# A hybrid decoder trunk on one core: byte distances of split weights, and a shorter lead of the slabs that are split ahead of a norm

## The chip, the cores and the metric

The kernel runs on 1 core of one Trainium2 chip. The metric is the device time of one execution in microseconds (us). The engines are named as the profile names them: PE is TensorE's matmul, PEld its weight load, DVE is VectorE, ACT is ScalarE, POOL is GpSimd, SP is SyncE, which issues most DMAs.

## The reference

`x` is 256 tokens x 1024 features. There are two layers of three sub-layers each: a SwiGLU FFN, a mixer, another FFN. Layer 0's mixer is a hybrid of a state-space scan and forgetting attention; layer 1's is a gated linear recurrence.

```python
def swiglu(x, w_in, w_out):                       # w_in 1024 x 5632, w_out 2816 x 1024
    gate, up = jnp.split(x @ w_in, 2, axis=-1)
    return (jax.nn.silu(gate) * up) @ w_out

def recurrent_mixer(h, w_in, conv_w, conv_b, w_a, b_a, w_x, b_x, lam, w_out):
    gate, xr = jnp.split(h @ w_in, 2, axis=-1)
    gate = jax.nn.gelu(gate, approximate=True)
    xr = causal_conv(xr, conv_w, conv_b)
    return (rg_lru(xr, w_a, b_a, w_x, b_x, lam) * gate) @ w_out

# every sub-layer, with weight 0.5 for the FFNs and 1 for the mixers
x = x + weight * rms_norm(f(rms_norm(x, g_pre)), g_post)
```

The hybrid mixer projects h to z, xbc, dt, q, k, v and f with one matrix of 1024 x 5656, runs a chunked scan on the first three and 8 attention heads on the others, and projects the 2048 results back with `hyb_w_out`.

## The kernel before

**Products from parts.** A float32 operand is split in two float32r parts: hi is the rounded copy, lo the rest. A product is hi x hi + hi x lo + lo x hi, three matmuls of 128 x 128 stationary columns and up to 512 moving columns. ACT makes hi (`act.copy`, L268), DVE makes lo (L269).

**Slabs.** All weights come as slabs of 128 x 1024 (512 KB) in the order in which they are used (`order`, built from `plans`). SP loads a slab into one of five `raw` buffers (L249), then `prepare` splits it into a slot of `w`. A slot holds the hi part from its first element and the lo part `pitch` elements further (L263 to L266). There are seven slots; later output slabs go to a pool of the phase. `slabs` splits 5 or 6 slabs beyond those that an operation needs (`LOOKAHEAD`), unless a norm is under way.

**Activations.** `xT` holds the normed activations transposed, per feature block a hi and a lo part of 256 tokens each. In the built program `xT` begins at byte 25760 of each partition and the seven slots of `w` at 62624 and every 8704 bytes on. All of these leave 160 when divided by 256.

**Phases.** The six sub-layers run one after another. An FFN has 22 feature tiles f. The first three (`NA`) are done per token tile t = 0, 1 with `xT` stationary (kind A). From f = 3 on (kind B, `b_tiles`) the weights are stationary: 2 matmuls hi x (hi and lo), 512 columns; 16 lo x hi, 256 columns; 14 hi x (hi and lo). After each B come output steps of earlier tiles (kind O, `out_step`), 6 matmuls of 512 columns per token tile. The hybrid mixer has 8 tiles with `xT` stationary (V, `a_one`) and 36 slabs with the weights stationary (XBC, Z, Q, K, `b_one`), 24 matmuls of 256 columns each. The recurrent one has 8 of the first kind (RA) and 8 of the second (GATE).

**The end of a phase.** Output steps of token tile 0 come first; then `finish` records tile 0's post-norm, its residual sum and the next phase's pre-norm (L331 squares on ACT, L379, L382 and L347 on DVE, two small steps on POOL), while PE does the deferred output steps of tile 1. Before the norm, `finish` splits the slabs of the next phase's first 2 x NA operations, which are the six slabs of f = 0, 1, 2, and makes the norm's instructions stand behind the last split on each engine (`behind(..., firsts)`). Later on PE transposes the normed tile (L143), and ACT and DVE write it into `xT` (L312).

**Order.** PE's order is that of the code. On the other engines a scheduler orders the recorded instructions by priority; `tc.high_priority(offset=...)` brings some forward.

**The recurrence.** `lru(n0)` handles four of eight blocks. After the square root it multiplies (L948), scans (L950), applies GELU to the gate (L953), multiplies by it (L954) and splits the result into a slot of `w`, called `two` (L955 to L956), for the output steps. It does so first for n0 = 0, then for n0 = 4.

Of the kernel before, what the change touches and what calls it, by code (L numbers as in the profile page):

```python
# [8 lines left out]
F32 = mybir.dt.float32  # L9
F32R = mybir.dt.float32r  # L10
# [6 lines left out]
P = 128  # L17
# [8 lines left out]
NEG = -1e30  # L26
SLAB = 1024

STEP, PLACES = 8, 16

NA = 3
BEHIND = 2
# [70 lines left out]
def slabs_of(op):  # L103
    kind, ph = op[0], op[1]
    if kind in ("A", "B", "V", "RA"):
        return [(kind if kind in ("V", "RA") else "I", ph, op[2], j) for j in range(2)]
    if kind in ("DTF", "XBC", "Z", "Q", "K", "GATE", "O"):
        return [(kind, ph, op[2])]
    return []
# [6 lines left out]
def hybrid_trunk(ctx: ExitStack, tc: tile.TileContext, x_in, norm_g, ffn_in, ffn_out,  # L116
# [119 lines left out]
    def behind(ins, firsts):  # L236

        for h in firsts:
            if h.ins.engine == ins.ins.engine:
                tc.add_manual_dep(ins.ins, h.ins.name, mybir.DependencyInfo(  # L240
                    mybir.DependencyClass.NoSync, mybir.DependencyReason.DATA), reason="norms and splits in turn")
        return ins
# [9 lines left out]
    def prepare(n):  # L252
        while ready[0] < min(n, len(order)):
            key = order[ready[0]]
            late = is_late(key)
            if late and key[1] not in pools:
                break
            ready[0] += 1
            load(ready[0])
            raw, width = loaded[ready[0] - 1]  # L260
            slots = SPLIT if not late else 7 if PHASES[key[1]][0] == "ffn" else LATE[PHASES[key[1]][0]]

            pitch = SLAB + (STEP * (key[2] % PLACES) if key[0] == "I" and key[2] >= NA else 0)  # L263
            full = (pools[key[1]] if late else wp).tile([P, 2 * SLAB + (0 if late else STEP * PLACES)], F32R, name="w", bufs=slots)
            w = full[:, 0:2 * SLAB].rearrange("p (j c) -> p j c", j=2)
            w = [full[:, 0:SLAB], full[:, pitch:pitch + SLAB], w]  # L266
            c = slice(0, width)
            splits[:] = [behind(act.copy(w[0][:, c], raw[:, c]), hold)]  # L268
            splits.append(behind(dve.tensor_tensor(w[1][:, c], raw[:, c], w[0][:, c].bitcast(F32), op=ALU.subtract), hold))  # L269
            split[key] = w  # L270
            load(ready[0] + RAW)
# [86 lines left out]
        norms.discard((ph, t))  # L358
        normed.add((ph, t))

    def new_xT():
        return res.tile([P, KT, 2, NT * P], F32R, name="xT")

    def finish(ph, t, acc, weight):

        xt = xs[t]
        last = ph == len(PHASES) - 1
        upto = [where[k] for op in (plans[ph + 1][:2 * NA] if not last else []) for k in slabs_of(op)]
        prepare(max(upto, default=0) + 1)
        with tc.high_priority(offset=400):  # L370
            firsts = splits + hold
            ms = mean_square(acc, weight, firsts)
            r = work.tile([P, 1], F32, name="r", bufs=4)
            rstd_of(r, ms, weight)
            hg = []
            for h in range(2):
                cols = slice(h * 512, (h + 1) * 512)
                hg.append(work.tile([P, 512], F32, name="xn", bufs=3))
                behind(dve.tensor_tensor(hg[h], acc[h], state["g_post"][:, cols], op=ALU.mult), firsts)  # L379
            for h in range(2):  # L380
                cols = slice(h * 512, (h + 1) * 512)
                dve.scalar_tensor_tensor(  # L382
                    xt[:, cols], hg[h], r, xt[:, cols], op0=ALU.mult, op1=ALU.add)
                if last:
                    (sp, act)[h].dma_start(out[t * P:(t + 1) * P, cols], xt[:, cols])
        if not last:
            if t == 0:
                state["xT_next"] = new_xT()
            spawn(pre_norm(ph + 1, t, state["xT_next"], LAG["norm"]))

    gsrc = [(0, 0), (0, 2), (0, 4), (1, 0), (1, 2), (1, 4)]
# [60 lines left out]
        hold[:] = latest.values()  # L452
        start_pool.__exit__(None, None, None)

    xT = new_xT()
    first_norms(xT)

    def out_step(accs, k, t, n, act_hl, w, halves=(0, 1)):
# [153 lines left out]
    def run_hyb(ph, plan, xT, mp):  # L612
# [5 lines left out]
        act.dma_start(gs, ssm_g)  # L618
        cs = mp.tile([P, 64], F32, name="cs")
        dt = mp.tile([P, NT, 24], F32, name="dt")  # L620
        dec = mp.tile([P, HEADS], F32, name="dec")
        rows = tc.dram_tile([24, 256], F32, name="rows")

        at_pool = tc.tile_pool(name="at", bufs=1)
# [259 lines left out]
    def run_rec(ph, plan, xT, mp):  # L884
# [31 lines left out]
        def lru(n0):  # L916
# [28 lines left out]
                yield 0.5  # L945

            rooted[n0] = behind(act.activation(r, r, func=AF.Sqrt, scale=0.25), [squared[4]])
            dve.tensor_tensor(r, r, i, op=ALU.mult)  # L948
            for j in range(4):
                dve.tensor_tensor_scan(i[:, j, :], a[:, j, :], r[:, j, :], 0.0, op0=ALU.mult, op1=ALU.add)  # L950
            while ("gate", n0 + 3) not in done or 4 not in rooted:
                yield 0.5
            behind(act.activation(gt[:, nn, :], gt[:, nn, :], func=AF.Gelu_apprx_tanh), [rooted[4]])  # L953
            dve.tensor_tensor(gt[:, nn, :], gt[:, nn, :], i, op=ALU.mult)  # L954
            two = wp.tile([P, 2, 4, 256], F32R, name="w", bufs=SPLIT)  # L955
            split_to(two[:, 0, :, :], two[:, 1, :, :], gt[:, nn, :])  # L956
            parts.update((n0 + j, [two[:, k, j, :] for k in range(2)]) for j in range(4))
            done.update(("out", n) for n in range(n0, n0 + 4))

# [115 lines left out]
```

## Time and profile before

| what | value |
|---|---|
| time, median of 3 runs | 1052.2 us (1052.01 to 1052.62) |
| time of the profiled execution | 1055.53 us |
| its span in the profile | 1053.3 us |
| TensorE busy | 1035.5 us, 98% |
| VectorE, ScalarE busy | 719.0 us (68%), 597.6 us (57%) |
| DMA | 195.90 MB, mean 186 GB/s |
| matmuls of 256 columns, xT moving | 2272 |
| matmuls of 512 columns, xT moving | 1216 |

[...] What a matmul costs is read from start to start.

### The profile page before, as it was taken

The numbers are of one execution on the slowest core, as the hardware profiler recorded it, in microseconds if no ns is written. First come the engines' busy times: TensorE is split into PE (matmuls) and PEld (weight loads), VectorE is DVE, ScalarE is ACT, GpSimd is POOL, SyncE is SP. The second block draws the span as 40 slices with busy tenths as digits, with TensorE's granted clock in tenths as the row PEclk, the third lists the DMA queues.
The fourth block names the chain that finished last, engine by engine and source line by source line (L and its number), as shares of the span: only waits on it lengthen the run. The fifth ranks groups of instructions, "written<-read, shape, count | busy, mean of one in ns | idle before, by whom it ended". The sixth has DMA issues, their size and how long they took to land.

```text
span 1053.3 us, 16022 instructions
## 1 busy us (share of the span) xinstructions
PE 1035.5 (98%) x6084; PEld 911.4 (87%) x6084; DVE 719.0 (68%) x1156; ACT 597.6 (57%) x1060; POOL 24.5 (2%) x60
## 2 busy tenths in 40 slices
PE   8999999999999999999999999999999989999997
PEld 7888888999999988888888888888899878888886
DVE  7766557589888776855557685555769858655563
ACT  6755456455565566645546564454659847545551
POOL 1000000100000001000000100000010010000000
PEclk9999999999999999999999999999999999999999
DMA  7966656265645472856556285555735446665521
GB/s 270 319 215 193 195 185 211 68 229 178 207 148 160 139 251 98 297 194 194 185 180 220 81 294 189 181 193 193 229 107 190 146 160 239 217 200 177 187 81 40
DMA packets 55745, 195.90 MB, mean 186 GB/s; under 512 B 6972, under 2 KB 8148, under 8 KB 55668
## 3 DMA queue, kind: packets, MB, share of 16 engines
q1 hardware_dynamic: 52464, 190.04, 55.3%
q10 hardware_dynamic: 3204, 4.84, 1.4%
q8 instruction: 47, 0.77, 0.3%
q14 instruction: 30, 0.25, 0.1%
HBM read 193.78 MB, written 1.07 MB: 185 GB/s over the span
## 4 chain that ended last, share of the span: by engine, by line
PE 88%; DVE 4%; ACT 4%; issue 2%; POOL 1%; DMA 1%; POOLq 0%; DVEq 0%; ACTq 0%
PE rot L139 56%; PE side L139 31%; ACT junk L331 1%; ACT w L268 1%; PE rot L143 1%; DVE c L600 1%; DVE w L269 1%; DMA raw<-in_ffn_out_dram 1%; POOL r L320 0%; DVE xn L347 0%; ACT xT L312 0%; DVE sc L950 0%; DVE x L382 0%; PE side L143 0%; POOL r L319 0%
## 5 line engine op out<-in xcount | busy, mean ns | idle before, releaser
L139 PE MATMUL rot<-xT,w 128*128 128x256 f32 (+1 forms) x3512 | 570.6, 320 | 0.0
L269 DVE TENSOR_TENSOR w<-raw,w 128x1024 fp32r<-128x1024 f32 (+1 forms) x349 | 423.1, 1218 | 200.7 <-ACT w L268 200.0
L139 PEld LDWEIGHTS rot<-xT,w 128*128 128x128 f32 x3512 | 503.0, 189 | 51.9 <-issue 1.3
L268 ACT CAST w<-raw 128x1024 fp32r<-128x1024 f32 (+1 forms) x349 | 364.9, 1050 | 169.6 <-DMA raw<-in_ffn_out_dram 143.3
L139 PE MATMUL side<-w,hid 128*128 128x512 f32 x1056 | 253.6, 390 | 0.0
L139 PEld LDWEIGHTS side<-w,hid 128*128 128x128 f32 x1056 | 197.4, 188 | 41.3
L139 PE MATMUL rot<-w,xT 128*128 128x256 f32 (+1 forms) x768 | 118.9, 313 | 0.9 <-DVE sg L285 0.5
L139 PEld LDWEIGHTS rot<-w,xT 128*128 128x128 f32 x768 | 105.0, 190 | 10.3 <-DVE sg L285 2.3
L312 ACT CAST hid<-up 128x256 fp32r<-128x256 f32 x76 | 30.9, 406 | 99.0 <-DVE up L567 99.0
L284 ACT COPY half<-rot 128x256 f32<-128x256 f32 x176 | 63.5, 363 | 17.3 <-PE rot L139 17.3
L285 DVE TENSOR_TENSOR sg<-rot,half 128x256 f32<-128x256 f32 x100 | 41.9, 419 | 15.2 <-ACT half L284 15.2
L312 DVE TENSOR_TENSOR hid<-up,hid 128x256 fp32r<-128x256 f32 x76 | 32.2, 424 | 29.1 <-ACT hid L312 29.1
L139 PE MATMUL side<-w,os 128*128 128x512 f32 x192 | 46.2, 396 | 0.0
L565 ACT ACTIVATE sg<-sg 128x256 f32<-128x256 f32 x76 | 31.7, 417 | 23.7 <-DVE sg L285 23.7
L139 PEld LDWEIGHTS side<-w,os 128*128 128x128 f32 x192 | 35.6, 188 | 7.9
L285 DVE TENSOR_TENSOR up<-rot,half 128x256 f32<-128x256 f32 x76 | 31.8, 419 | 3.1 <-ACT half L284 3.1
L567 DVE TENSOR_TENSOR up<-sg,up 128x256 f32<-128x256 f32 x76 | 31.8, 419 | 0.2
L379 DVE TENSOR_TENSOR xn<-side,g_post 128x512 f32<-128x512 f32 x24 | 16.5, 691 | 21.2 <-ACT junk L331 20.8
L331 ACT ACTIVATE junk<-side 128x512 bf16<-128x512 f32 x24 | 14.3, 597 | 23.8 <-PE side L139 22.9
L319 POOL TENSOR_SCALAR r<-ms 128x1 f32<-128x1 f32 x24 | 7.2, 300 | 870.7 <-ACT junk L331 864.8
L347 DVE SCALAR_TENSOR_TENSOR xn<-x,r,g_pre 128x512 f32<-128x512 f32 x20 | 14.2, 750 | 16.8 <-POOL r L320 16.8
L139 PE MATMUL side<-w 128*128 128x512 f32 x96 | 23.2, 400 | 1.1 <-DVE w L312 1.1
(195 smaller groups left out, 509.3 us busy)
## 6 DMA issues: line engine op xcount, KB each, us to landing
raw<-in_ffn_in_dram SPq DMA_DIRECT2D x176, 512.0 KB, 4.5
raw<-in_ffn_out_dram SPq DMA_DIRECT2D x88, 512.0 KB, 4.7
raw<-in_hyb_cols_dram SPq DMA_DIRECT2D x36, 512.0 KB, 4.2
raw<-in_hyb_out_dram SPq DMA_DIRECT2D x16, 512.0 KB, 3.6
raw<-in_hyb_v_dram SPq DMA_DIRECT2D x8, 512.0 KB, 4.7
raw<-in_rec_a_dram SPq DMA_DIRECT2D x8, 512.0 KB, 4.7
raw<-in_rec_cols_dram SPq DMA_DIRECT2D x8, 512.0 KB, 3.9
raw<-in_rec_out_dram SPq DMA_DIRECT2D x8, 512.0 KB, 3.6
```

Source lines behind the costliest of these rows:

```text
L139: pe.matmul(ps, lhsT=lhsT, rhs=rhs, start=start, stop=stop)
L143: pe.transpose(ps, src, ident)
L268: splits[:] = [behind(act.copy(w[0][:, c], raw[:, c]), hold)]
L269: splits.append(behind(dve.tensor_tensor(w[1][:, c], raw[:, c], w[0][:, c].bitcast(F32), op=ALU.subtract), hold))
L284: act.copy(tmp, ps[:, 256:512])
L285: dve.tensor_tensor(dst, ps[:, 0:256], tmp, op=ALU.add)
L312: return act.copy(hi, src), dve.tensor_tensor(lo, src, hi.bitcast(F32), op=ALU.subtract)
L331: behind(act.activation(junk, src, func=AF.Square, scale=1.0 / (32.0 * weight), accum_out=ms[:, h:h + 1]), firsts)
L347: dve.scalar_tensor_tensor(xn[h], xt[:, cols], r, state["g_pre"][:, cols], op0=ALU.mult, op1=ALU.mult)
L379: behind(dve.tensor_tensor(hg[h], acc[h], state["g_post"][:, cols], op=ALU.mult), firsts)
L565: act.activation(sg, sg, func=AF.Silu)
L567: dve.tensor_tensor(up, sg, up, op=ALU.mult)
```

## The change

There are five edits. (1) The lo part of every FFN slab from f = 3 on lies 56 elements beyond the plain pitch, in place of 8 x (f mod 16). The lo parts of Z, XBC, Q, K and GATE lie 32 elements beyond it, in place of 0. (2) `xT` is 128 elements longer; in the two mixers its contents begin 48 elements in. (3) `dec` is padded from 64 to 512 bytes, so that the tiles behind it in the hybrid mixer begin at other bytes: `os`, the split inputs of the output steps, at remainder 160 modulo 256 in place of 224, and the late output slabs at 160 in place of 224 as well. (4) At the end of the recurrent mixer `finish` asks for the slabs of the next two operations (f = 0 and 1), not six. (5) In `lru(0)` the product, the scans, the GELU, the product with the gate and the split get a high priority, and the last three go in halves of two blocks.

```diff
-STEP, PLACES = 8, 16
+LINES = 128
+
+OFF = {"I": 56, "Z": 32, "XBC": 32, "Q": 32, "K": 32, "GATE": 32}
+OFF_MIXER = 48
...
-            pitch = SLAB + (STEP * (key[2] % PLACES) if key[0] == "I" and key[2] >= NA else 0)
-            full = (pools[key[1]] if late else wp).tile([P, 2 * SLAB + (0 if late else STEP * PLACES)], F32R, name="w", bufs=slots)
+            pitch = SLAB + (0 if key[0] == "I" and key[2] < NA else OFF.get(key[0], 0))
+            full = (pools[key[1]] if late else wp).tile([P, 2 * SLAB + (0 if late else LINES)], F32R, name="w", bufs=slots)
...
-    def new_xT():
-        return res.tile([P, KT, 2, NT * P], F32R, name="xT")
+    def new_xT(ph):
+        n, e = KT * 2 * NT * P, 0 if PHASES[ph][0] == "ffn" else OFF_MIXER
+        return res.tile([P, n + LINES], F32R, name="xT")[:, e:e + n].rearrange("p (k j c) -> p k j c", k=KT, j=2)
...
-        upto = [where[k] for op in (plans[ph + 1][:2 * NA] if not last else []) for k in slabs_of(op)]
+        ahead = 2 * NA if PHASES[ph][0] != "rec" else NA - 1
+        upto = [where[k] for op in (plans[ph + 1][:ahead] if not last else []) for k in slabs_of(op)]
...
-        dec = mp.tile([P, HEADS], F32, name="dec")
+        dec = mp.tile([P, 2 * HEADS + 96], F32, name="dec")[:, 0:HEADS]
...
-            dve.tensor_tensor(r, r, i, op=ALU.mult)
-            for j in range(4):
-                dve.tensor_tensor_scan(i[:, j, :], a[:, j, :], r[:, j, :], 0.0, op0=ALU.mult, op1=ALU.add)
+            with tc.high_priority(offset=URGENT if n0 == 0 else 0):
+                dve.tensor_tensor(r, r, i, op=ALU.mult)
+                for j in range(4):
+                    dve.tensor_tensor_scan(i[:, j, :], a[:, j, :], r[:, j, :], 0.0, op0=ALU.mult, op1=ALU.add)
...
-            behind(act.activation(gt[:, nn, :], gt[:, nn, :], func=AF.Gelu_apprx_tanh), [rooted[4]])
-            dve.tensor_tensor(gt[:, nn, :], gt[:, nn, :], i, op=ALU.mult)
-            two = wp.tile([P, 2, 4, 256], F32R, name="w", bufs=SPLIT)
-            split_to(two[:, 0, :, :], two[:, 1, :, :], gt[:, nn, :])
+            with tc.high_priority(offset=URGENT if n0 == 0 else 0):
+                two = wp.tile([P, 2, 4, 256], F32R, name="w", bufs=SPLIT)
+                for j in range(0, 4, 2 if n0 == 0 else 4):
+                    js, ns = slice(j, j + (2 if n0 == 0 else 4)), slice(n0 + j, n0 + j + (2 if n0 == 0 else 4))
+                    behind(act.activation(gt[:, ns, :], gt[:, ns, :], func=AF.Gelu_apprx_tanh), [rooted[4]])
+                    dve.tensor_tensor(gt[:, ns, :], gt[:, ns, :], i[:, js, :], op=ALU.mult)
+                    split_to(two[:, 0, js, :], two[:, 1, js, :], gt[:, ns, :])
```

The order of the instructions on PE, POOL and SP is the same before and after. On ACT and DVE it changes in the recurrent mixer and at the start of the FFN behind it, at two places.

The first place is ACT at the end of the recurrent mixer, before the change: `w<-raw` are splits of slabs, `junk,ms<-side` the squares of a token tile's output sums, `junk,ms<-x` those of its pre-norm (`x_83` is token tile 0), and `xT<-rot` the copies behind the transposes.

```order
L312 CAST w<-gt 128x1024
L268 CAST w<-raw 128x1024 x6
L331 ACTIVATE junk,ms<-side 128x512 x2
L331 ACTIVATE junk,ms<-x_83 128x512 x2
L312 CAST xT<-rot 128x4x128 x2
L331 ACTIVATE junk,ms<-side 128x512 x2
```

The same place after the change:

```order
L315 CAST w<-gt 128x1024
L271 CAST w<-raw 128x1024 x5
L334 ACTIVATE junk,ms<-side 128x512 x2
L334 ACTIVATE junk,ms<-x_83 128x512 x2
L315 CAST xT<-rot 128x4x128 x2
L271 CAST w<-raw 128x1024
L334 ACTIVATE junk,ms<-side 128x512 x2
```

One split of six has moved from ahead of tile 0's norm to between tile 0's copies and tile 1's norm; DVE's order shows the same move.

The second place is DVE behind the square root, before the change: `sc` rows of 128x256 are the scans (those into `sc_8379` of blocks 0 to 3, those into `sc_8506` of blocks 4 to 7), `gt<-gt,sc` the product with the gate, `w<-gt,w` the lo part of `two`.

```order
L950 SCALAR_TENSOR_TENSOR sc_8379<-sc_8380,sc_8378 128x256
L950 SCALAR_TENSOR_TENSOR sc_8506<-sc_8507,sc_8505 128x256 x4
L950 SCALAR_TENSOR_TENSOR sc_8379<-sc_8380,sc_8378 128x256 x3
L269 TENSOR_TENSOR w<-raw,w 128x1024
L954 TENSOR_TENSOR gt<-gt,sc_8379 128x1024
L269 TENSOR_TENSOR w<-raw,w 128x1024 x2
L312 TENSOR_TENSOR w<-gt,w 128x1024
L269 TENSOR_TENSOR w<-raw,w 128x1024 x2
L954 TENSOR_TENSOR gt<-gt,sc_8506 128x1024
L269 TENSOR_TENSOR w<-raw,w 128x1024 x2
L312 TENSOR_TENSOR w<-gt,w 128x1024
```

And after it:

```order
L957 SCALAR_TENSOR_TENSOR sc_8379<-sc_8380,sc_8378 128x256 x4
L965 TENSOR_TENSOR gt<-gt,sc_8379 128x512
L957 SCALAR_TENSOR_TENSOR sc_8506<-sc_8507,sc_8505 128x256 x3
L965 TENSOR_TENSOR gt<-gt,sc_8379 128x512
L315 TENSOR_TENSOR w<-gt,w 128x512
L957 SCALAR_TENSOR_TENSOR sc_8506<-sc_8507,sc_8505 128x256
L272 TENSOR_TENSOR w<-raw,w 128x1024
L315 TENSOR_TENSOR w<-gt,w 128x512
L272 TENSOR_TENSOR w<-raw,w 128x1024 x5
L965 TENSOR_TENSOR gt<-gt,sc_8506 128x1024
L272 TENSOR_TENSOR w<-raw,w 128x1024
L315 TENSOR_TENSOR w<-gt,w 128x1024
```

The lo part of blocks 0 to 3 comes in two halves, with one slab's split ahead of the second, where three stood ahead of the whole; six slabs' splits stand ahead of the product of blocks 4 to 7, where five stood.

## Rows read from the trace of the kernel before

**Rows 1.** The page's head: span, and TensorE's busy time, share and instructions.

```profile
span 1053.3 us, 16022 instructions
PE 1035.5 (98%) x6084; PEld 911.4 (87%) x6084; DVE 719.0 (68%) x1156; ACT 597.6 (57%) x1060; POOL 24.5 (2%) x60
```

**Rows 2.** Timeline, PE, first FFN: start us, us, instructions; f = 4, 7, 8, 12.

```profile
43.37 5.73 PE L139 MATMUL rot<-xT,w 128*128 128x512 f32 x32
...
57.24 2.88 PE L139 MATMUL side<-w,hid 128*128 128x512 f32 x12
59.96 5.74 PE L139 MATMUL rot<-xT,w 128*128 128x512 f32 x32
...
68.25 5.69 PE L139 MATMUL rot<-xT,w 128*128 128x512 f32 x32
...
76.50 5.73 PE L139 MATMUL rot<-xT,w 128*128 128x512 f32 x32
...
109.59 5.73 PE L139 MATMUL rot<-xT,w 128*128 128x512 f32 x32
```

**Rows 3.** Timeline, PE, hybrid mixer: a run of 132, and what follows.

```profile
225.76 16.00 PE L139 MATMUL rot<-xT,w 128*128 128x256 f32 x132
241.60 0.52 PE L139 MATMUL side<-d,upper 128*128 128x24 f32 x4
```

**Rows 4.** Timeline, PE, cut to the 16 short matmuls: f = 8, 10, 14, 16.

```profile
76.73 2.30 PE L139 MATMUL rot<-xT,w 128*128 128x512 f32 x17
...
93.31 2.27 PE L139 MATMUL rot<-xT,w 128*128 128x512 f32 x17
...
126.41 2.27 PE L139 MATMUL rot<-xT,w 128*128 128x512 f32 x17
...
142.94 2.30 PE L139 MATMUL rot<-xT,w 128*128 128x512 f32 x17
```

**Rows 5.** Timeline, PE, end of the recurrent mixer; brackets: idle before, releaser.

```profile
833.06 0.63 PE L139 MATMUL side<-w 128*128 128x512 f32 x2
834.78 20.24 PE L139 MATMUL side<-w 128*128 128x512 f32 x88 [1.09 <-DVE w L312]
858.62 1.97 PE L143 MATMUL rot<-ident,xn 128*128 128x128 f32 x8 [3.59 <-DVE xn L347]
...
862.44 6.93 PE L139 MATMUL rot<-w,xT 128*128 128x512 f32 x41
```

**Rows 6.** Timeline, ACT, end of the recurrent mixer.

```profile
850.98 1.05 ACT L268 CAST w<-raw 128x1024 fp32r<-128x1024 f32 x1 [5.21 <-PE side L139]
```

**Rows 7.** Windows: stretch, its us, busy of PE to POOL, PEclk, DMA share, GB/s.

```profile
858.50:862.00 3.50, 3.38 (x13) 3.06 (x14) 2.11 (x4) 1.19 (x3) 0.00 (x0) 0.52 0.00 0
```

**Rows 8.** Timeline, PE, the hybrid mixer's output steps and the next FFN's start.

```profile
371.47 3.05 PE L139 MATMUL side<-w,os 128*128 128x512 f32 x12
374.35 0.83 PE L139 MATMUL rot<-pT,v 128*128 128x128 f32 x6
374.94 29.33 PE L139 MATMUL side<-w,os 128*128 128x512 f32 x126
404.11 1.04 PE L143 MATMUL rot<-ident,xn 128*128 128x128 f32 x8
...
406.36 6.93 PE L139 MATMUL rot<-w,xT 128*128 128x512 f32 x41
```

**Rows 9.** Timeline, DVE, both mixers' ends.

```profile
411.95 1.42 DVE L347 SCALAR_TENSOR_TENSOR xn<-x,r,g_pre 128x512 f32<-128x512 f32 x2 [1.24 <-POOL r L320]
...
824.31 4.76 DVE L950 TENSOR_TENSOR_SCAN sc<-sc,sc 128x256 f32<-128x256 f32 x8
...
841.46 5.75 DVE L269 TENSOR_TENSOR w<-raw,w 128x1024 fp32r<-128x1024 f32 x5
...
852.07 1.22 DVE L269 TENSOR_TENSOR w<-raw,w 128x1024 fp32r<-128x1024 f32 x1 [4.85 <-ACT w L268]
```

More of the change, by code (lines that the diff above doesn't have):

```diff
@@ L387, in finish @@
             if t == 0:
-                state["xT_next"] = new_xT()
+                state["xT_next"] = new_xT(ph + 1)
             spawn(pre_norm(ph + 1, t, state["xT_next"], LAG["norm"]))
@@ L453, in first_norms @@
         start_pool.__exit__(None, None, None)
-    xT = new_xT()
+    xT = new_xT(0)
     first_norms(xT)
```

## The prediction

> **What bounds the kernel now.** I read the head of the page first: TensorE is busy for 1035.5 of 1053.3 us [rows 1]. So the end moves only where the pace of the matmuls changes or where TensorE stands still. I then read TensorE in order of time, and last the engines it waits for.
>
> *Pace.* A turn of the FFN is 32 matmuls of one feature tile (2 of 512 columns, 16 of 256, 14 of 512) and 12 of an output step. The 12 take 59.96 - 57.24 = 2.72 us, 226.7 ns each, so a 256-column one at that pace would take 113.3 [rows 2]. It does not: in the hybrid mixer 132 of them take 241.60 - 225.76 = 15.84 us, 120.0 ns each [rows 3]. Nothing is waited for there; these matmuls are simply slow.
>
> *What sets the pace.* Every turn has the same matmuls, yet turns differ. By "distance" I mean the byte of the stationary operand minus the byte of the moving one, modulo 256. The built program puts xT and all slots of w at remainder 160, so before the change tile f has its lo part at distance 32 x (f mod 8). Tile 7 (224 bytes) goes from start to start in 76.50 - 68.25 = 8.25 us; the eight turns from tile 4 to tile 12 go through all eight distances and take 109.59 - 43.37 = 66.22 us, 0.22 more than eight turns of 8.25 [rows 2]. Cut out alone, the 16 short matmuls with the one before them take 2.30 us at distance 0 (tile 8) and 2.27 at 64 (tile 10) and 192 (tile 14); tile 16, whose lo part lies 256 bytes from tile 8's, again takes 2.30, which is why I count modulo 256 [rows 4].
>
> *Standstills.* Two are in reach of the change, both in the recurrent mixer: 1.09 us before the third output matmul, for the lo part of the gated hidden state, and 3.59 us before the transposes that lead to the last FFN, for the pre-norm of token tile 0 [rows 5]. That norm is late for one reason: the sixth split of an FFN slab stands ahead of it on ScalarE, and waits 5.21 us for a slot that output steps on TensorE still read; it starts at 850.98 [rows 6]. [...]
>
> **Part 1: one distance for FFN slabs.** No instruction is added or moved. All 19 tiles from f = 3 get distance 224. Eight turns give back 0.22 us; a phase has two such eights, then tile 20 (a turn like tile 4's) and 21: about 0.55 us. Four phases: 2.2 us, all on the path, since TensorE follows itself there. This is the surest term, as tiles 7 and 15 of every phase run so already.
>
> **Part 2: two distances for the mixers.** xT moves by 192 bytes. Where weights are stationary, the hi part is then at distance 64 and the lo part, 128 bytes further out, at 192; each run of three goes hi, hi, lo. Where xT is stationary (V, RA) it is 192 throughout. The hybrid mixer has 36 slabs x 24 = 864 of the first kind and 8 x 24 = 192 of the second; the recurrent one 192 and 192. From 2.30 and 2.27 over 16 matmuls, 64 and 192 each save 0.03 / 16 = 1.9 ns, rounded to 2. What the trace does not show is an alternation of two distances. Its bounds: the full 6.7 ns down to 113.3, and a loss up to 13 ns, the most that a steady run at an unfavourable distance shows (12 output matmuls of the hybrid mixer, 374.35 - 371.47 = 2.88 us, 240 ns against 226.7 [rows 8]). I take 2 ns, since both distances alone give it. Hybrid: 1056 x 2 = 2.1 us, 2.0 after what waits on ScalarE there take back. Recurrent RA: 192 x 2 = 0.4, of which I count 0.2, since the convolutions on VectorE are waited for soon after. The gates' share is swallowed by the wait in part 4.
>
> [...]
>
> **Part 3: `dec` padded to 512 bytes.** It carries nothing; it moves the hybrid's `os` tiles from remainder 224 to 160, so output steps read at distance 0, as the FFN's do. The 126 in one run take 404.11 - 374.94 = 29.17 us [rows 8], against 126 x 226.7 = 28.56; 0.6 us, and about 0.2 for the shorter runs ahead: 0.8 us (0 to 1.4).
>
> **Part 4: the gated hidden state in halves.** For the first four blocks the gate's product and its split come in halves of 512 columns, and the scans of the first half go first. On VectorE the first lo half now comes after seven scans of 0.6 us, two half products and itself (a whole instruction takes 1.22, a half about 0.7): 824.31 + 4.2 + 2.0 = 830.5 [rows 9]. TensorE asks for it two matmuls after 833.06, so the 1.09 us go. What is late next is the other half (blocks 4 to 7): it stays behind the same raw splits. Its lo part ends at 841.46, where the five raw splits begin [rows 9]; with four half instructions in place of two whole, and some slips, I put it at 841.9. TensorE reaches the matmul that needs it (36 after 834.78, at 226.7 ns) at 842.94 now, and could reach it at about 841.2. So it waits 0.7 us there, and 842.9 - 841.9 = 1.0 us is gained in all.
>
> **Part 5: fewer slabs ahead of the norm.** The lookahead has already split five of the six slabs; with the bound at two feature tiles, the sixth goes behind token tile 0's norm on ScalarE and VectorE. The five end on VectorE at 841.46 + 5.75 = 847.2, in the new order at 847.65. The last output matmul of tile 0 is the 58th after 834.78: 847.9 now, 846.9 then. So VectorE decides: its norm starts at 847.65 instead of behind the sixth split, 852.07 + 1.14 = 853.2 [rows 9]. That is 5.5 us earlier, and the transposes' data is there at 858.6 - 5.5 = 853.1. TensorE still has the deferred steps of tile 1 to do: 88 x 226.7 ns after 834.78 is 854.73, less 1.0: 853.75. No standstill is left; the transposes start 4.87 us earlier. At full clock the eight transposes and six matmuls take 406.36 - 404.11 = 2.25 us (hybrid to FFN, [rows 8]); here they take 862.44 - 858.62 = 3.82 [rows 5]. Another 1.57: the next FFN starts 6.4 us earlier.
>
> What is late next: the moved split now stands between tile 0's xT copies and tile 1's norm. A cast of 1.05 us [rows 6] pushes that norm by up to as much; the new order gives about 0.3 back, since a copy no longer stands between the norm's two squares on ScalarE. In the same place after the hybrid mixer the norm's data is ready at 411.95 + 1.42 = 413.4 [rows 9], and TensorE asks 41 matmuls after 406.36 [rows 8], which here take 6.93 with the last one's tail [rows 5]: 413.3, no slack. I charge 0.6. Parts 4 and 5 together: 1.0 + 3.9 + 1.57 - 0.6 = 5.8 us (4 to 7).
>
> **Sum.** 2.2 + 2.0 + 0.2 + 0.8 + 5.8 = 11.0 us. The profiled execution took 1055.5 us, 2.2 of it outside the span; 1055.5 - 11.0 = 1044.5. It stands 3.3 above the median of the runs, 1052.2, so I expect **1041.2 us**.
>
> **Rivals.**
> A. The alternation does better than either distance alone and brings 256-column matmuls near 113.3: 1056 x 6.7 = 7.1 instead of 2.0, and a little in RA. 1036. For it: runs of distance 224 do mix fast and slow; against it: neither 64 nor 192 does.
> B. In the mixers only the stationary operand's own byte counts, not the distance, or the alternation undoes the gain. Weights then stand at remainders 160 and 32, which FFN tiles with xT fixed cannot tell from distances 0 and 128. 1043.4.
> C. Distances are worth nothing in any phase, and the turns differ by something that goes with the tile's number. Then only parts 4 and 5 are left: 1052.2 - 5.8 = 1046.4. [...] Against it: the same pace returns with the residue in [rows 4].
> D. The norm is not freed: the five splits or their loads slip and TensorE stands still as before at the transposes, with the clock drop. The 5.4 us of that place go: 1046.6. Against it: VectorE is through at 847.2 in the trace.
> E. The other side. Every change of distance between hi and lo costs as much as the 240 ns steps do, 13 ns a matmul. In the hybrid mixer: 1056 x 13 = 13.7 us lost in place of 2.0 gained, 1041.2 + 15.7 = 1057, slower. It decides from (11.0 - 2.0) / 1056 = 8.5 ns a matmul on. For it: a distance of 64 is bad in those 512-column steps; against it: at 256 columns the same 64 is better than 0 [rows 4].
>
> **Chances.** Forecast 0.62, A 0.12, B 0.13, C 0.02, D 0.07, E 0.04. A and D end the range, 1035.5 to 1047, which leaves out E and the tails. No change means within 0.2%, 2.1 us, about what a measurement of this kernel can tell from none: only a mixture near 8 ns a matmul in E or several failures at once, 0.02; slower 0.03; faster 0.95.
>
> **What would show it.** Part 1: every turn from tile 4 on takes 8.25 us. Part 2: the run of 132 takes 15.6 us rather than 15.84 (15.0 for A, above 16 for E). Part 3: the run of 126 takes 28.6. Part 4: no wait for the first lo half, a short one some 36 matmuls later. Part 5: the first norm of the mixer's end on ScalarE directly behind five casts, no idle before the transposes, and a granted clock of 1.0 there; then a wait of some 0.5 us before the transposes of tile 1. I am wrong if the runs of 132 do not move, or if TensorE still stands still for microseconds at the transposes.

## The result, and the profile after

| kernel | median us | runs | lowest to highest | ratio to before, 95% interval |
|---|---|---|---|---|
| before | 1052.28 | 4 | 1052.01 to 1052.62 | |
| after | 1037.44 | 4 | 1037.07 to 1038.97 | 0.9861 [0.9849, 0.9874] |

The change takes 14.8 us away. The forecast was 11.0 us (1041.2 us) with a range of 1035.5 to 1047. The measured time lies inside it, but nearer to rival A's 1036 than to the forecast.

The profiled execution of after took 1037.15 us, close to its median, while that of before took 1055.5, 3.3 above its own. These two executions therefore differ by 18.4 us, and some 3 us of that are not the change: before's execution lost them at its start. The windows view shows it; its columns are the stretch, its us, busy us of PE, PEld, DVE, ACT and POOL, granted clock as a share of full speed, DMA share, GB/s. First the kernel before, then after:

```profile
0.00:14.00 14.00, 10.11 (x47) 8.26 (x47) 6.79 (x15) 7.46 (x15) 3.37 (x11) 0.88 0.80 284
8.50:12.00 3.50, 3.08 (x14) 3.08 (x15) 3.42 (x7) 2.02 (x4) 0.91 (x3) 0.51 1.00 406
```

```profile
0.00:14.00 14.00, 10.88 (x60) 8.86 (x61) 8.54 (x17) 9.83 (x18) 3.38 (x11) 1.00 0.83 307
8.50:12.00 3.50, 3.50 (x31) 3.33 (x31) 3.50 (x6) 3.20 (x6) 0.72 (x2) 1.00 1.00 401
```

In the same 3.5 us TensorE got through 14 matmuls at a granted clock of 0.51 in the one and 31 at 1.00 in the other. In before the first FFN begins 2.26 us later, and then takes 0.86 us more than its turns explain. So I compare stage by stage, from the first matmul of one to the first of the next (us); the third FFN (0.57 less) and the other tiles of the last one (0.59 less) go as the second does:

| stage | before | after | less |
|---|---|---|---|
| second FFN | 185.15 | 184.57 | 0.58 |
| hybrid mixer | 207.63 | 201.68 | 5.95 |
| recurrent mixer, RA | 29.22 | 28.47 | 0.75 |
| gates 0 and 1, convolutions | 9.71 | 9.92 | -0.21 |
| the gates' run of 144 | 17.46 | 16.53 | 0.93 |
| output products up to token tile 0's sums | 15.01 | 15.06 | -0.05 |
| deferred products of tile 1, then the standstill | 10.55 | 6.81 | 3.74 |
| transposes and six products | 3.82 | 2.25 | 1.57 |
| first tiles of the last FFN | 18.38 | 18.64 | -0.26 |

The page's head answers to [rows 1]: TensorE is busy for 13.5 us less and the span is 17.9 shorter.

```profile
span 1035.4 us, 16026 instructions
PE 1022.0 (99%) x6084; PEld 898.7 (87%) x6084; DVE 718.3 (69%) x1158; ACT 598.8 (58%) x1062; POOL 24.6 (2%) x60
```

TensorE in order of time, first FFN of after, answers to [rows 2]. Columns: start us, us, instructions with their count, and in brackets idle time before and what ended it.

```profile
40.24 5.69 PE L142 MATMUL rot<-xT,w 128*128 128x512 f32 x32
45.77 2.88 PE L142 MATMUL side<-w,hid 128*128 128x512 f32 x12
48.49 5.69 PE L142 MATMUL rot<-xT,w 128*128 128x512 f32 x32
54.02 2.88 PE L142 MATMUL side<-w,hid 128*128 128x512 f32 x12
56.74 5.69 PE L142 MATMUL rot<-xT,w 128*128 128x512 f32 x32
```

Every turn with 12 output matmuls is now 8.25 us from start to start, the value read from tile 7 of before. The same view in the mixers answers to [rows 3] and to the run of 126 in [rows 8]; the third row is the gates' run:

```profile
221.41 15.17 PE L142 MATMUL rot<-xT,w 128*128 128x256 f32 x132
236.42 0.52 PE L142 MATMUL side<-d,upper 128*128 128x24 f32 x4
...
365.75 28.86 PE L142 MATMUL side<-w,os 128*128 128x512 f32 x126
394.45 1.03 PE L146 MATMUL rot<-ident,xn 128*128 128x128 f32 x8
...
804.26 16.69 PE L142 MATMUL rot<-xT,w 128*128 128x256 f32 x144
```

A row's busy time runs past the next row's start (221.41 + 15.17 = 236.58 us, against 236.42), so paces are taken from start to start. The run of 132 takes 236.42 - 221.41 = 15.01 us, 113.7 ns a matmul, where the forecast had 15.6 and rival A 15.0. The run of 126 takes 394.45 - 365.75 = 28.70 us, where it had 28.6.

The recurrent mixer's end answers to [rows 5]:

```profile
820.79 8.34 PE L142 MATMUL side<-w 128*128 128x512 f32 x36
829.29 0.73 PE L142 MATMUL side<-w 128*128 128x512 f32 x2 [0.17 <-ACT w L315]
830.74 12.08 PE L142 MATMUL side<-w 128*128 128x512 f32 x52 [0.71 <-DVE w L315]
842.66 1.03 PE L146 MATMUL rot<-ident,xn 128*128 128x128 f32 x8
843.45 1.62 PE L142 MATMUL side<-w 128*128 128x512 f32 x6
844.91 6.92 PE L142 MATMUL rot<-w,xT 128*128 128x512 f32 x41
852.02 1.29 PE L146 MATMUL rot<-ident,xn 128*128 128x128 f32 x8 [0.18 <-DVE xn L350]
```

The wait for the first lo half is gone. New ones stand before the second half, 0.17 us for its hi part and 0.71 us for its lo part. The transposes wait for nothing, and those of tile 1 wait 0.18 us. ScalarE and VectorE at that place answer to [rows 6, 9], and the window around the transposes to [rows 7]:

```profile
834.46 1.06 ACT L271 CAST w<-raw 128x1024 fp32r<-128x1024 f32 x1 [0.19 <-DMA raw<-in_ffn_in_dram]
835.44 0.60 ACT L334 ACTIVATE junk<-side 128x512 bf16<-128x512 f32 x1
```

```profile
830.60 6.17 DVE L272 TENSOR_TENSOR w<-raw,w 128x1024 fp32r<-128x1024 f32 x5
...
841.33 1.42 DVE L350 SCALAR_TENSOR_TENSOR xn<-x,r,g_pre 128x512 f32<-128x512 f32 x2 [1.99 <-POOL r L323]
```

```profile
842.00:845.50 3.50, 3.50 (x23) 3.05 (x22) 2.18 (x5) 2.20 (x4) 0.00 (x0) 1.00 0.00 0
```

The post-norm's first square follows the fifth cast on ScalarE directly, without the split that waited 5.21 us there. The pre-norm's last two products run from 841.33 to 842.75. The transposes begin at 842.66 without a wait, while the second of them is still running, so hardly any slack is left. TensorE has no idle time there and the clock stays at 1.00, where it was 0.52.

### The profile page after: what moved, and what is told of

Read it like the earlier page. It is cut to its first block, busy times and chain, and to the rows that moved or that the text cites. A ratio compares the mean times of both kernels' runs of the same rounds, so it can differ in the third digit from the quotient of the medians.

```text
span 1035.4 us, 16026 instructions
## 1 busy us (share of the span) xinstructions
PE 1022.0 (99%) x6084; PEld 898.7 (87%) x6084; DVE 718.3 (69%) x1158; ACT 598.8 (58%) x1062; POOL 24.6 (2%) x60
## 4 chain that ended last, share of the span: by engine, by line
PE 89%; DVE 4%; ACT 3%; issue 2%; DMA 1%; POOL 1%; DVEq 0%; POOLq 0%; ACTq 0%
PE rot L142 57%; PE side L142 31%; PE rot L146 1%; DVE c L606 1%; ACT junk L334 1%; ACT w L271 1%; DVE w L272 1%; DMA ca<-rows 0%; DMA raw<-in_rec_out_dram 0%; POOL r L323 0%; DVE sc L957 0%; DVE xn L350 0%; DVE x L388 0%; POOL r L322 0%; DVE sc L955 0%
## 5 line engine op out<-in xcount | busy, mean ns | idle before, releaser
L142 PE MATMUL rot<-xT,w 128*128 128x256 f32 (+1 forms) x3512 | 562.1, 318 | 0.0
L142 PEld LDWEIGHTS rot<-xT,w 128*128 128x128 f32 x3512 | 494.6, 187 | 51.9 <-issue 1.3
L288 DVE TENSOR_TENSOR sg<-rot,half 128x256 f32<-128x256 f32 x100 | 41.9, 419 | 13.5 <-ACT half L287 13.2
```

The lines of the kernel that those rows point to most:

```text
L142: pe.matmul(ps, lhsT=lhsT, rhs=rhs, start=start, stop=stop)
L288: dve.tensor_tensor(dst, ps[:, 0:256], tmp, op=ALU.add)
```

## The experiments

Every kernel is the kernel after with the edit shown. "Distance" is as in the prediction.

### The mixers' part undone, and one constant distance in its place

```diff
 # e1_mix0
-OFF = {"I": 56, "Z": 32, "XBC": 32, "Q": 32, "K": 32, "GATE": 32}
-OFF_MIXER = 48
+OFF = {"I": 56}
+OFF_MIXER = 0
 # e2_mix64: the first line as in e1_mix0, OFF_MIXER = 48
 # e3_mix192: the first line as in e1_mix0, OFF_MIXER = 16
```

With no mixer offsets (e1_mix0):

> The changed kernel with the mixers' distances undone: xT begins at its first element in every phase and the lo parts of Z, XBC, Q, K and GATE lie at the plain pitch, so that all distances in the mixers are 0 again; FFN distance 224, the padded dec and the recurrent mixer's order stay. If the distances alone made the mixers' pace (their 256-column matmuls go at 113.3 to 114 ns in the changed kernel's trace, 120 before), it returns to 120 ns: 1056 x 6.4 = 6.8 us in the hybrid mixer and up to 1 us in the recurrent one, 1044 to 1045.5 us. If the pace came from anything else that the change moved (the size of xT, the slots' bytes, dec), nothing changes: 1037.4.

Constant distance 64 (e2_mix64):

> The changed kernel with lo parts of Z, XBC, Q, K and GATE at the plain pitch: hi and lo both at distance 64, no alternation; V and RA stay at 192. Theory 'alternation': two distances in turn are what brings 113.3 ns; a constant 64 gives the 117.7 that FFN tiles at 64 show, 864 x 4.2 = 3.6 us more in the hybrid mixer, 1041 us. Theory 'settling': a long run of 256-column matmuls reaches 113.3 at any distance but 0 and 128, and an FFN's run of 16 does not because it begins in the state that the 512-column ones leave: no change, 1037.4 us.

Constant distance 192 (e3_mix192):

> The changed kernel with xT 64 bytes in, not 192, in the mixers, and lo at the plain pitch: the slabs with stationary weights at a constant 192, V and RA at a constant 64. Theory 'alternation': 117.7 ns for the slabs, 1041 us, while V keeps 113.5. Theory 'settling': 113.3 to 114 in all, 1037.4 us. Theory 'distance alone, as in the FFN': 117.7 in all of the hybrid mixer, 1056 x 4.2 = 4.4 us more, 1042 us.

| kernel | median us | lowest to highest | ratio to before | hybrid stage us |
|---|---|---|---|---|
| after | 1037.44 | 1037.07 to 1038.97 | 0.9861 [0.9849, 0.9874] | 201.68 |
| e1_mix0 | 1043.10 | 1042.87 to 1043.58 | 0.9909 [0.9895, 0.9924] | 207.02 |
| e2_mix64 | 1038.28 | 1037.60 to 1038.68 | 0.9862 [0.9848, 0.9877] | 202.14 |
| e3_mix192 | 1038.71 | 1038.33 to 1038.80 | 0.9866 [0.9850, 0.9883] | 203.20 |

Part 2 is worth 5.7 us by the medians, a little less than expected: the hybrid stage gives 5.34 us, which is 5.1 ns for each of its 1056 matmuls and not 6.4. In e1_mix0 the run of 132 is back where it was in [rows 3], and the gates' run too:

```profile
222.03 16.00 PE L142 MATMUL rot<-xT,w 128*128 128x256 f32 x132
...
810.27 17.61 PE L142 MATMUL rot<-xT,w 128*128 128x256 f32 x144
```

One distance alone gets most of it (1038.3 and 1038.7 us, where the theory of alternation had 1041), which neither the 2 ns of the forecast nor the idea that only the alternation helps foresaw. What it misses is seen where one stretch is compared between kernels. A run of 96 that starts at 241.99 in after, at 241.87 in e2_mix64:

```profile
241.99 11.15 PE L142 MATMUL rot<-xT,w 128*128 128x256 f32 x96
```

```profile
241.87 11.56 PE L142 MATMUL rot<-xT,w 128*128 128x256 f32 x96
```

and in e3_mix192 the run of 132 and the gates' run:

```profile
220.92 15.12 PE L142 MATMUL rot<-xT,w 128*128 128x256 f32 x132
...
805.67 17.31 PE L142 MATMUL rot<-xT,w 128*128 128x256 f32 x144
```

At a constant 64 or 192 a run holds one of two steady paces to its end. Start to start, a matmul takes 113.3 ns in the one and 117.7 in the other: e3_mix192 has the first in its run of 132 and the second in the gates' run (17.31 against 16.69 in after, 0.62 / 144 = 4.3 ns each). In the hybrid mixer, from the run of 132 on, about three quarters of the times from start to start with the weights stationary are 113 or 114 ns in e2_mix64 (587 of 782 that are 113, 114, 117 or 118), and 244 of 754 in e3_mix192. In after none of these runs of 36 or more stays at the slow pace: after about ten matmuls it is at 113.3.

What decides between the two paces at a constant distance stays open, but it is not the distance or the bytes alone. Where xT is stationary, the kernel after has a constant 192 too. The recurrent mixer has runs of 24 there, and e12_ffn88 (below) has every byte of them in the same place. Yet two runs in a row go at 113.3 and then 117.9 ns from start to start in after, and at 117.7 and then 113.3 in e12_ffn88 (first after, then e12_ffn88):

```profile
775.35 3.00 PE L142 MATMUL rot<-w,xT 128*128 128x256 f32 x24
...
778.32 3.07 PE L142 MATMUL rot<-w,xT 128*128 128x256 f32 x24
```

```profile
773.36 3.10 PE L142 MATMUL rot<-w,xT 128*128 128x256 f32 x24
...
776.43 2.97 PE L142 MATMUL rot<-w,xT 128*128 128x256 f32 x24
```

So the alternation reaches only the tiles with the weights stationary; with xT stationary the change leaves some runs at the slow pace (117.7 and 117.9 ns).

### All by 32 bytes further

```diff
-    power = const.tile([P, 1], F32, name="power")
+    power = const.tile([P, 16], F32, name="power")[:, 0:1]
```

> The changed kernel with a small constant tile padded so that x, xT, raw, w and all behind them begin 32 bytes further, at remainder 192 modulo 256 in place of 160. All distances stay. If only distances count: the same as the changed kernel, an FFN turn of 8.25 us, 226.7 ns for a 512-column matmul, 1037.4 us. If the operands' own remainders count (160 is 32 beyond a multiple of 64, 192 is one), the paces of 226.7 or 113.3 ns move, in either direction; 5 ns on 226.7 would be 13 us in all.

Measured: 1037.81 us (1037.21 to 1039.96), ratio 0.9862 [0.9848, 0.9877]; the run of 132 starts at 221.68 and the next matmul at 236.69, 15.01 us as in after. The bytes of both operands have moved by 32, their distance has not, and the time and the runs with the weights stationary stay: the distance counts, not either operand's own byte. This speaks against rival B. So does e2_mix64 beside e1_mix0: the weights stand at the same bytes in both, only xT has moved, and that gains 4.8 us. Why the distance counts, no run shows.

### The lookahead before the norm undone

```diff
-        ahead = 2 * NA if PHASES[ph][0] != "rec" else NA - 1
+        ahead = 2 * NA
```

> The changed kernel with six slabs again ahead of the norm at the end of the recurrent mixer. [...] Rival: the norm was freed by the recurrence's new order and by the quicker gates; then nothing changes, 1037.4.

Measured: 1042.75 us (1040.74 to 1044.16), ratio 0.9904 [0.9888, 0.9921]: 5.3 us lost, where part 5 of the prediction has 3.9 + 1.57 - 0.6 = 4.9. TensorE, ScalarE and the window around the transposes show the old standstill and its cause, as in [rows 5 to 7]:

```profile
846.39 1.97 PE L146 MATMUL rot<-ident,xn 128*128 128x128 f32 x8 [3.59 <-DVE xn L350]
848.01 2.35 PE L142 MATMUL side<-w 128*128 128x512 f32 x6
850.20 6.92 PE L142 MATMUL rot<-w,xT 128*128 128x512 f32 x41
```

```profile
838.75 1.05 ACT L271 CAST w<-raw 128x1024 fp32r<-128x1024 f32 x1 [3.36 <-PE side L142]
839.71 0.59 ACT L334 ACTIVATE junk<-side 128x512 bf16<-128x512 f32 x1
```

```profile
846.00:850.50 4.50, 4.11 (x16) 3.65 (x17) 2.40 (x5) 1.89 (x5) 0.00 (x0) 0.62 0.00 0
```

The sixth cast stands ahead of the norm and waits 3.36 us for TensorE; the transposes wait 3.59 us, and the granted clock is 0.62 in the window around them. So it is part 5 that removes the standstill, not the quicker gates or the new order of the recurrence, which this kernel still has.

### The old end of the recurrence, with and without the mixers' part

```diff
 # e6_lru: scans, gate product and split of the first four blocks as before the change
-            with tc.high_priority(offset=URGENT if n0 == 0 else 0):
-                dve.tensor_tensor(r, r, i, op=ALU.mult)
 ...
-                two = wp.tile([P, 2, 4, 256], F32R, name="w", bufs=SPLIT)
-                for j in range(0, 4, 2 if n0 == 0 else 4):
 ...
+            two = wp.tile([P, 2, 4, 256], F32R, name="w", bufs=SPLIT)
+            split_to(two[:, 0, :, :], two[:, 1, :, :], gt[:, nn, :])
 # e13_mix0_lru: e6_lru and e1_mix0 together
```

> The changed kernel with the recurrence's end in its old order (no priority, no halves). Forecast: the wait of 1.1 us before the third output matmul returns and the wait for blocks 4 to 7 (0.7 us) goes, and VectorE ends 0.5 us sooner: worth 1.0 us by the forecast, 1038.4. Rival: in the changed kernel's trace the two waits nearly cancel (1.27 us of gap before, 0.9 us now), so 0.4 us, 1037.8, within what can be told.

Measured for e6_lru: 1040.60 us (1039.93 to 1041.57), ratio 0.9886 [0.9871, 0.9901]: 3.2 us lost. Both expectations were too small, so I undid the mixers' part with it (e13_mix0_lru):

> The kernel after with both the mixers' distances undone (0 bytes, as in the run without them, 1043.1 us) and the old order of the recurrence's end (as in the run that undid it alone, 1040.6 us). The theory that the new order of the recurrence is worth more the sooner the gates' products are through, since VectorE's scans end at the same time either way: with the mixers at the old pace its undoing costs only what stands between the two traces at that pace, 9.6 - 8.2 = 1.4 us on the four pairs of first products, so 1044.5 us. The rival, that the two parts simply add: the undoing costs the 3.2 us that it cost in the kernel after, so 1046.3 us.

Measured for e13_mix0_lru: 1045.31 us (1044.74 to 1046.73), ratio 0.9932 [0.9919, 0.9946], 2.2 us above e1_mix0, between the two numbers. The traces are plainer. From the start of the gates' run to the transposes TensorE takes 39.29 us in e13_mix0_lru against 38.18 in e1_mix0, 1.1 more; and 40.89 in e6_lru against 38.40 in after, 2.5 more. So undoing it costs more with the mixers' part in. The medians have 0.7 and 1.1 us more; where that lies, these single executions do not show. TensorE in e6_lru and then in e13_mix0_lru:

```profile
820.72 0.73 PE L142 MATMUL side<-w 128*128 128x512 f32 x2 [0.17 <-ACT w L315]
823.04 21.86 PE L142 MATMUL side<-w 128*128 128x512 f32 x88 [1.59 <-DVE w L315]
844.73 1.03 PE L146 MATMUL rot<-ident,xn 128*128 128x128 f32 x8
```

```profile
829.68 20.27 PE L142 MATMUL side<-w 128*128 128x512 f32 x88 [1.10 <-DVE w L315]
849.78 1.03 PE L146 MATMUL rot<-ident,xn 128*128 128x128 f32 x8
```

The longer wait, 1.59 us in place of 1.10, is the smaller share, 0.5 us. The larger is in the 88 matmuls behind it: 844.73 - 823.04 = 21.69 us against 849.78 - 829.68 = 20.10. The windows there, e6_lru first and e13_mix0_lru second, say why:

```profile
823.00:826.00 3.00, 2.96 (x7) 2.33 (x8) 3.00 (x3) 2.36 (x3) 0.00 (x0) 0.54 0.95 284
```

```profile
830.00:834.00 4.00, 4.00 (x19) 3.27 (x18) 4.00 (x4) 2.90 (x3) 0.00 (x0) 1.00 0.92 308
```

Behind the longer wait the granted clock is 0.54 in this execution: eight matmuls take 427 ns each, start to start, in place of 226.7, 1.6 us. Behind the shorter one it stays at 1.00. The reason given for the theory, that VectorE's scans end at the same time and so the wait grows, therefore explains the smaller part, 0.5 us; the clock behind the wait costs 1.6.

### The FFN at the mixers' two distances

```diff
-OFF = {"I": 56, "Z": 32, "XBC": 32, "Q": 32, "K": 32, "GATE": 32}
+OFF = {"I": 32, "Z": 32, "XBC": 32, "Q": 32, "K": 32, "GATE": 32}
 ...
-        n, e = KT * 2 * NT * P, 0 if PHASES[ph][0] == "ffn" else OFF_MIXER
+        n, e = KT * 2 * NT * P, OFF_MIXER
```

> The changed kernel with the mixers' distances in the FFNs too: hi at 64, lo at 192, and 192 where xT is stationary. Theory: at a constant 64 or 192 a run of 256-column matmuls has two paces, 113.3 and 117.7 ns, by how it begins; 512-column ones at distance 64 went at 233 to 240 ns in the hybrid mixer of before, against 226.7 at 0. So the 16 short ones may fall to 113.3 (16 x 3.3 x 76 = 4.0 us less, 1033) but the 28 long ones that a turn would have at 64 rise by 6 to 13 (at 12 of 16 turns' matmuls 76 x 14 x 6 = 6.4 us more at least): 1040 to 1050 us. Rival: long matmuls also have a quick state at 64, then 1033.

Measured: 1045.54 us (1044.85 to 1045.82), ratio 0.9931 [0.9916, 0.9946]: 8.1 us lost. A turn of the first FFN:

```profile
90.50 5.77 PE L142 MATMUL rot<-xT,w 128*128 128x512 f32 x32
98.87 5.77 PE L142 MATMUL rot<-xT,w 128*128 128x512 f32 x32
```

8.37 us in place of 8.25. The hi products of 512 columns take 233.0 ns on average from start to start at distance 64 (229.3 at 0 in after). The short lo ones take 117.7 at 192 (116.6 at 224): they did not fall to 113.3, as the theory allowed. The 12 output products of a turn, whose own distance is still 0, take 230.2 ns each where they took 226.7, so part of the loss falls on matmuls that only stand behind the slow ones. So the distances that suit the mixers' 256-column matmuls (113.7 ns each in after's run of 132) do not suit the 512-column ones here (233.0 ns against 229.3).

### The output steps without the padding of `dec`

```diff
-        dec = mp.tile([P, 2 * HEADS + 96], F32, name="dec")[:, 0:HEADS]
+        dec = mp.tile([P, HEADS], F32, name="dec")
```

> The kernel after without the 128 floats of padding behind `dec`, so that the outputs `os` of the hybrid mixer stand where they stood before the change. The theory that distances alone count: the 186 matmuls of the out steps go back from 227.8 ns each to 231.5, 3.7 x 186 = 0.7 us, so about 1038.1 us against 1037.4 of the kernel after, and no other stage moves. The rival, that the padding only changed where later tiles stand and the out steps were faster for another reason: they stay at 227.8 ns, and the time at 1037.4.

Measured: 1037.58 us (1037.05 to 1039.76), ratio 0.9860 [0.9842, 0.9878]. The 186 output matmuls take 231.4 ns on average against 227.8, 186 x 3.6 = 0.67 us, as expected; this is the only evidence. The hybrid stage takes 202.09 us, but it takes from 201.39 to 202.41 in the eight kernels that have after's hybrid mixer, and the medians are only 0.14 us apart, with runs 2.7 us apart. So neither the stage nor the whole time can show it.

### Every fourth byte of distance in the FFN, and the two best

```diff
 # e10_survey: a new distance for each FFN tile from f = 3, all multiples of 4 in turn
+            if key[0] == "I" and key[2] >= NA:
+                pitch = SLAB + (19 * {0: 0, 2: 1, 3: 2, 5: 3}[key[1]] + key[2] - NA) % 64
 # e11_ffn180
-OFF = {"I": 56,
+OFF = {"I": 45,
 # e12_ffn88
-OFF = {"I": 56,
+OFF = {"I": 22,
```

> The changed kernel with the lo part of the n-th FFN tile (f from 3 on, phases counted through, n from 0 to 75) 4 x (n mod 64) bytes beyond the plain pitch: every distance that is a multiple of 4 once, the first twelve twice, at other tile numbers than before. If the distance sets a turn's time, the 32 matmuls take 5.567, 5.573, 5.540, 5.533, 5.567, 5.580, 5.573, 5.527 us at 0, 32, ... 224 bytes, whatever the tile; if the tile's number does, they follow f as before. Between the multiples of 32 nothing is known; some may be better than 5.527.

The 32 matmuls of a turn, start to start, in the survey (1041.13 us, one run):

| distance, bytes | 180 | 88 | 208 | 28, 44, 212 | 224 | 96 | 64 | 0, 128 | 32, 192 | 160 | 52 | 204 |
|---|---|---|---|---|---|---|---|---|---|---|---|---|
| us | 5.480 | 5.487 | 5.507 | 5.520 | 5.527 | 5.534 | 5.540 | 5.567 | 5.573 | 5.580 | 5.606 | 5.627 |

The table shows a choice of the 64. The eight multiples of 32 came out at the times expected from the distance, to 0.001 us (0 in the second of its two turns), and all but 160 at other tile numbers than before. Twelve distances come twice, with another tile number. Ten of them agree within 0.001 us; at distance 4 the two differ by 0.033, and at 0 one turn is longer by 0.081. That turn is the first of its phase, and the first is longer by 0.09 us in after too; so the readings at 76, 152 and 228, which stand first in the other phases, are too long as well and are left out. So the turn's time goes with the distance, and rival C falls. The best turn and its neighbour at 184:

```profile
663.55 5.64 PE L142 MATMUL rot<-xT,w 128*128 128x512 f32 x32
671.75 5.74 PE L142 MATMUL rot<-xT,w 128*128 128x512 f32 x32
```

At 180 the sixteen short matmuls settle at 113.3 ns from the third on; at 204 they take 121 and 126 in turn. I took the two best to the whole kernel:

> The kernel after with the second half of each FFN input slab 180 bytes further than a whole multiple of 256, in place of 224. The theory that a distance fixes the pace of a run of 16, whatever tile it is: the 32 matmuls of one B tile took 5.480 us at this distance in the survey against 5.527 in the kernel after, so 76 turns x 0.047 = 3.6 us less: 1033.9 us. The rival, that a run of 16 settles on its fast or its slow steady pace by how it began, and that the one reading of 5.480 us was a lucky beginning: the turns spread between about 5.48 and 5.55 us, and the time lies between 1035.5 and 1038.

> The same with 88 bytes. The theory that a distance fixes the pace: 5.487 us for the 32 matmuls of a B tile in the survey, so 76 x 0.040 = 3.0 us less than the kernel after: 1034.4 us. The rival, a lucky beginning of the one run read: turns that spread over 5.48 to 5.55 us, 1035.5 to 1038 us.

| kernel | median us | lowest to highest | ratio to before |
|---|---|---|---|
| after | 1037.44 | 1037.07 to 1038.97 | 0.9861 [0.9849, 0.9874] |
| e11_ffn180 | 1035.45 | 1033.91 to 1036.55 | 0.9835 [0.9820, 0.9850] |
| e12_ffn88 | 1034.67 | 1034.28 to 1036.62 | 0.9832 [0.9818, 0.9847] |

The turns came out as the survey had them: 71 of 76 take 5.480 us in e11_ffn180, and 71 of 76 take 5.486 or 5.487 in e12_ffn88, so one reading of one turn was not luck. From start to start a turn of e11_ffn180 is 8.20 us:

```profile
83.28 5.64 PE L142 MATMUL rot<-xT,w 128*128 128x512 f32 x32
91.48 5.64 PE L142 MATMUL rot<-xT,w 128*128 128x512 f32 x32
```

Its four FFN phases are 3.2 us shorter than in after, and those of e12_ffn88 2.8 us (forecast 3.6 and 3.0). By the medians e11_ffn180 gains only 2.0, at the edge of what its rival expected, though the turns do not spread as the rival has it. Its profiled execution, the slowest of the four (1036.55), has before's slow start (granted clock 0.88 in the first 14 us, 1.9 us) and a hybrid stage 0.7 us longer, of which 0.3 is a new wait. Whether the fastest one, 1033.91, is free of such losses, no trace shows. e12_ffn88 is the fastest kernel here by its median, 2.8 us below after, with intervals that do not overlap. Which of the two is better, these runs cannot tell.

## Why the prediction came out as it did

The forecast was short by 3.8 us, and one term, part 2, holds nearly all of it. Rival A, at 0.12, came closer in time (1036) and had the better size for that term.

- **Part 1, 2.2 us: right.** All turns but four take 5.526 or 5.527 us for their 32 matmuls; the second, third and fourth FFN are 0.57 to 0.59 us shorter, 2.3 in all. The step from [rows 2] to 8.25 us holds. The choice of 224 among multiples of 32 was read rightly as the best of those; that finer steps have better ones was outside the prediction.
- **Part 2, 2.2 us: the mechanism was right, the size wrong.** It measures 5.7 us. The step that failed is "I take 2 ns, since both distances alone give it": the trace of before shows 64 and 192 only in runs of 16 behind 512-column matmuls, and there they go at 117.7 ns, as the 16 at 192 do in e8_ffn_as_mix. In long runs the same two distances can reach 113.3 (e2_mix64, e3_mix192), and in alternation every run of 36 or more does (after). So long runs come to the upper bound that the prediction named, 6.7 ns; over the hybrid stage, with its beginnings of runs and its tiles with xT stationary, 5.1 ns are left of it, 5.3 us where the forecast had 2.0 and rival A 7.1. RA gives 0.75, of which 0.2 is lost again at the convolutions. Rival A's reason was half right: distance alone brings most of it, and the alternation keeps long runs from the slow pace. That is worth 0.8 and 1.3 us by the medians against constant 64 and 192, about what the runs differ by. In the hybrid stage it is 1.5 us against 192; the 0.46 against 64 is within what that stage differs by between kernels, and only single runs like the 96 above show it.
- **The gates' share, counted as nothing: right.** Their run is 0.93 us shorter and the waits behind it grow by about as much, 1.1 us: from e1_mix0 to after, the output products up to tile 0's sums go from 13.93 to 15.06 us.
- **Part 3, 0.8 us: right.** 0.67 us by the rows (e9_dec); too small for the medians.
- **Part 4, 1.0 us: right at the pace it was worked out for.** e13_mix0_lru against e1_mix0 shows 1.1 us in the trace. With the mixers' pace of the kernel after it is worth 2.5 us there and 3.2 by the medians, because without it the wait grows (1.59 us in e6_lru) and the granted clock behind it is 0.54. The wait for the second half was foreseen, but that its size agrees (0.7 us; 0.71 came) is luck. Its 841.2 is 36 matmuls from 833.06, which leaves out the two ahead of the old wait: 833.06 us + 38 x 226.7 ns is 841.67 us, and the wait that is left is 0.2 us. The 1.0 us does not rest on it. At the pace of before the 90 matmuls take 848.46 - 827.73 = 20.73 us in e1_mix0, only 0.33 above 90 x 226.7 ns, so no wait of 0.7 us is in them; it comes in after because the gates' run ends 0.93 us sooner. The rows of e1_mix0:

```profile
827.73 20.89 PE L142 MATMUL side<-w 128*128 128x512 f32 x90
848.46 1.07 PE L146 MATMUL rot<-ident,xn 128*128 128x128 f32 x8
```

- **Part 5, 3.9 + 1.57 - 0.6 us: right.** At the old pace, from the stages of e1_mix0 against before, the standstill brings 3.75, the clock 1.53, and the last FFN's first tiles give 0.17 back, less than the 0.6 charged: tile 1's transposes wait 0.18 us. The stretch that the prediction takes for full clock, 404.10 to 406.36 us of before, has a granted clock of 1.00; the one at the transposes has 0.52 [rows 7]. Undoing part 5 costs 5.3 us.
- **Rivals.** B falls by e4_shift32, by e2_mix64 beside e1_mix0, and by the 5.7 us that are lost with the offsets in e1_mix0. C falls by the survey and by e1_mix0, which has the same matmuls as after and is 5.7 us slower. D falls by the trace: no idle before the transposes. E falls as a price for alternation; but e8_ffn_as_mix shows that a distance of 64 does cost time at 512 columns, about 4 ns a matmul.

The terms as measured: 2.3 + 5.7 + 0.7 + 1.1 + 5.1 = 14.9 us, against 14.8 between the medians.

## What to carry to other kernels

Where a matmul is slower than its neighbours of the same shape with nothing waited for, look at the bytes at which the two operands stand (here modulo 256: 2.30 us at tiles 8 and 16 alike [rows 4]), and measure a sweep of distances in one run: here one tile per distance was enough, the first of a phase excepted. A pace read from short runs between other matmuls is no measure for long runs at the same distance: at a constant 64 it was 117.7 ns in the one and mostly 113.3 in the other. And price a wait together with the clock behind it: the same removed wait was worth 1.1 us at the mixers' old pace and 2.5 at the new one, where it was longer (1.59 us against 1.10) and the granted clock behind it was 0.54.

## What the runs showed of the hardware beyond that

- At a constant distance of 64 or 192 a long run of 256-column matmuls keeps to one of two paces, 113.3 or 117.7 ns, to its end, and runs with the same bytes took different ones in after and e12_ffn88. At distance 0 it goes at 120.0 (before, e1_mix0). With 64, 64, 192 in turn every run of 36 or more ended at 113.3.
- In the FFN the time of a turn's 32 matmuls is no smooth function of the distance: 180 gives 5.480 us, 184 gives 5.580, and 204 gives 5.627.
- After waits of 0.17 and 1.59 us with two matmuls between them the granted clock was 0.54 (e6_lru); after one of 1.10 us at the same place it stayed at 1.00 (e13_mix0_lru). Each is one execution.
